# Second group's square sums, first state keys and last head factors placed later among the products; no products of zeros; last results stored by pairs of tiles

## The chip, the core and the metric

The kernel runs on one core of a Trainium2 chip. The metric is the device time of one execution in microseconds; the time of a kernel is the median of its runs. Every duration below comes from one profiled execution, from the runs' times, or from what the trace of that execution answers.

The core has five engines with a queue each: TensorE (PE in the profile; its weight loads are PEld), VectorE (DVE), ScalarE (ACT), GpSimd (POOL) and SyncE (SP). An instruction waits at the head of its engine's queue until what it needs is there, and what stands behind it waits with it.

## What is computed

A decoder trunk of two layers over 16 meta tokens and 512 tokens, model width 1024, in float32:

```python
for layer in range(DEPTH):
    g = norm_gains[layer]
    h = h + 0.5 * rmsnorm(swiglu(rmsnorm(h, g[0]), w_ffn_in[layer, 0], w_ffn_out[layer, 0]), g[1])
    hn = rmsnorm(h, g[2])
    if layer < N_A_LAYERS:
        mix = gla_mixer(hn, ...)                      # chunked gated linear attention, 4 heads
    else:
        mix = swa_mixer(hn, ..., k_sh, v_sh, cos, sin)  # sliding window of 128, 16 query heads, 4 key heads
    h = h + rmsnorm(mix, g[3])
    h = h + 0.5 * rmsnorm(swiglu(rmsnorm(h, g[4]), w_ffn_in[layer, 1], w_ffn_out[layer, 1]), g[5])
    if layer == N_A_LAYERS - 1:
        k_sh, v_sh = shared_kv(h, g_kv, w_kv, cos, sin)
return h[:, N_META:]
```

`rmsnorm` divides a row by the root of its mean square; `swiglu` is `(silu(gate) * up) @ w_out` with an inner width of 2816. The gated linear attention cumulates a gate per key channel, and each head's output goes through an `rmsnorm` of its own before it is gated and projected.

## The kernel before

**Layout.** Everything is held transposed: channels on the 128 partitions, tokens along the free dimension. The residual stream H and the work area Y are eight tiles of 128 channels by 528 tokens. Tokens come in two groups: in layer 0 `L0`, of 272 and 256 tokens; in layer 1 `L1`, of 256 and 256 (the meta tokens are dropped there), or `L1W`, one group of 512.

**Products.** A weight and an operand are each split into a high and a low float32r part, and a product is made of three matmuls: high by high, low by high, high by low. `mm3` (L344) does this for one output and `mm3s` (L333) for several outputs at once.

**Order of the work.** The program is written out by a small planner, `Flow` (L60). Jobs are Python generators; `yield 1.5` puts a job to sleep for 1.5 of the planner's clock. The clock moves with the products: `mm` (L161) adds n / 2400 for a float32r matmul of n columns and max(n / 600, 0.12) for any other. After a product, `flow.pump()` writes out each job that has come due. So a `yield` decides after how many products a job's instructions stand in TensorE's queue. A scheduler behind the planner may still exchange instructions that it takes to be not yet ready. `flow.wait` lets the clock run with no products until a job is done.

**Stages.** First FFN of layer 0 (names l0f0), gated linear attention (l0m), second FFN (l0f1), shared keys and values (kv), first FFN of layer 1 (l1f0), window attention (l1m), second FFN (l1f1), output. In the profile the figures at the end of names are left out, so the FFNs of a layer are both l0f or l1f.

**`x_first` (L509)** opens each stage: four weight units are multiplied by the first token group of the operand, then by the second, so that the second group's operand may come later. With at most 256 tokens in the group, two units share one PSUM bank of 512 columns. Before the products each such bank is set to zero by one matmul of a zero weight with a zero operand (L532), and none of the products starts an accumulation. Groups of 256 take two such matmuls, groups of 272 none: four in the stages of layer 1, two in the stages of layer 0 and in kv, 20 in all.

**Square sums and factors.** `Residual.run` (L453) ends a stage for one group: it makes the factors of the post-norm, adds the result to H tile by tile, builds the next operand from each tile and sums its squares (`sumsq`, ACT squares and POOL adds). Then L469 spawns `factors` (L436) for the next operand: `yield FACT`, and `rstd` (L348). `rstd` multiplies the sums by a column of ones (tile `st`), computes 1/sqrt on POOL or DVE into a diagonal matrix `dg`, sleeps for CHAIN (5) or DCHAIN (3.0), and multiplies ones by `dg` to spread the factors (tile `r`). `factors` copies `r` into R, by which the stage's outputs are scaled when they leave their banks (`drain`, L515).

**Gated linear attention (`gla`, L782).** One `core` job per head, each after the one before it. It prepares decayed queries and keys on DVE and ACT, sleeps for STATE_KEYS (L889) and transposes the state keys `kf` on TensorE (tile `pk`, L893). At its end `scale` (L951) makes the head's factors by `rstd` (tiles `st_go`, `dg_go`, `r_go`) for both groups. Between the heads' steps run the products of the next units; eight units of the output gate close the stage and the output projection follows.

**Window attention (`swa`, L1060).** Queries are scaled by R and rotated as they leave their banks; then score, softmax and value jobs run for eight pairs of heads, with four more query units and, later, the output projection between them.

**Output (`store`, L471).** For each group, four steps of two tiles: DVE multiplies by the factors, DVE or POOL adds H, and SP issues one store for each of the two tiles (L481, L482).

## Time and profile before

| | us |
|---|---|
| median of 3 runs | 1934.42 (1931.07 to 1936.41) |
| the profiled execution | 1931.38 |
| its span | 1929.5 |
| TensorE busy in it | 1888.9 |

The span is the time from the first to the last instruction that the profile shows; the execution's own time has 1.9 us more around it. The granted TensorE clock was 0.996 of full speed over the span. A row of TensorE's timeline that merges many matmuls gives the time from the first start to the last end; a single matmul's duration is its way through the array, and several are under way at once, so the pace is read from start to start.

### The profile page before, as it was taken

The numbers are of one execution on the slowest core, as the hardware profiler recorded it, in microseconds if no ns is written. First come the engines' busy times: TensorE is split into PE (matmuls) and PEld (weight loads), VectorE is DVE, ScalarE is ACT, GpSimd is POOL, SyncE is SP. The second block draws the span as 40 slices with busy tenths as digits, with TensorE's granted clock in tenths as the row PEclk, the third lists the DMA queues.
The fourth block names the chain that finished last, engine by engine and source line by source line (L and its number), as shares of the span: only waits on it lengthen the run. The fifth ranks groups of instructions, "written<-read, shape, count | busy, mean of one in ns | idle before, by whom it ended". The sixth has DMA issues, their size and how long they took to land.

```text
span 1929.5 us, 37402 instructions
## 1 busy us (share of the span) xinstructions
PE 1888.9 (98%) x14522; PEld 1798.1 (93%) x14522; DVE 1420.1 (74%) x2868; ACT 1001.7 (52%) x2268; POOL 215.1 (11%) x417
## 2 busy tenths in 40 slices
PE   8999999999999999999999999999998999999997
PEld 7999999999999999999999898989976898989897
DVE  7885858676464788585887786868788779858584
ACT  5663636653245555353574453535645665636363
POOL 2000000321111400000033000000352140000002
PEclk9999999999999999999999999999999999999998
DMA  4332333322113123323351123233421212333331
GB/s 163 104 100 88 103 96 106 114 74 69 45 52 113 56 72 95 102 91 102 99 176 45 61 88 115 87 112 99 132 66 34 77 45 72 98 105 107 101 112 44
DMA packets 102144, 174.61 MB, mean 90 GB/s; under 512 B 11472, under 2 KB 24272, under 8 KB 101968
## 3 DMA queue, kind: packets, MB, share of 16 engines
q1 hardware_dynamic: 101680, 172.11, 28.2%
q8 instruction: 113, 1.85, 0.4%
q14 instruction: 63, 0.52, 0.1%
q10 hardware_dynamic: 288, 0.13, 0.0%
HBM read 170.10 MB, written 2.10 MB: 89 GB/s over the span
## 4 chain that ended last, share of the span: by engine, by line
PE 70%; DVE 19%; ACT 6%; issue 3%; POOL 1%; DMA 0%; SPq 0%; DVEq 0%; ACTq 0%; POOLq 0%
PE y L162 30%; PE x L162 16%; PE a L162 11%; DVE raw L251 5%; PE c L162 4%; DVE w_s L246 3%; DVE w L246 3%; ACT w_s L245 3%; PE d L162 2%; DVE w L227 2%; PE o L162 1%; ACT w L226 1%; PE po L162 1%; DVE hidl0f L775 1%; PE sc L162 0%
## 5 line engine op out<-in xcount | busy, mean ns | idle before, releaser
L246 DVE TENSOR_TENSOR w_s<-raw,w_s 128x512 fp32r<-128x512 f32 x288 | 194.0, 690 | 129.7 <-ACT w_s L245 127.6
L227 DVE TENSOR_TENSOR w<-raw,w 128x512 fp32r<-128x512 f32 x378 | 244.9, 673 | 31.1 <-ACT w L226 29.3
L162 PE MATMUL y<-hidl0f,w 128*128 128x256 f32 (+1 forms) x2112 | 261.0, 285 | 0.0
L162 PEld LDWEIGHTS y<-hidl0f,w 128*128 128x128 f32 x2112 | 258.8, 188 | 0.7
L245 ACT ACTIVATE w_s<-raw 128x512 fp32r<-128x512 f32 x288 | 175.3, 628 | 149.5 <-DVE raw L251 146.0
L162 PE MATMUL y<-hidl1f,w 128*128 128x512 f32 (+1 forms) x1344 | 249.8, 346 | 0.0
L162 PEld LDWEIGHTS y<-hidl1f,w 128*128 128x128 f32 x1344 | 212.0, 188 | 33.9 <-ACT hidl1f L774 0.4
L226 ACT ACTIVATE w<-raw 128x512 fp32r<-128x512 f32 x378 | 209.0, 586 | 46.0 <-PE y L162 39.4
L403 POOL TENSOR_TENSOR acc_post<-acc_post,sq_post 128x256 f32<-128x256 f32 (+1 forms) x72 | 56.9, 791 | 1386.5 <-ACT sq_post L402 1386.0
L251 DVE TENSOR_TENSOR raw<-raw,raw 128x512 f32<-128x512 f32 x288 | 198.0, 687 | 5.5
L246 DVE TENSOR_TENSOR w<-raw,w 128x512 fp32r<-128x512 f32 x216 | 148.3, 687 | 41.5 <-ACT w L245 40.2
L245 ACT ACTIVATE w<-raw 128x512 fp32r<-128x512 f32 x216 | 133.9, 621 | 48.0 <-PE y L162 47.7
L162 PE MATMUL x<-x_l0m,w 128*128 128x272 f32 (+1 forms) x1200 | 158.3, 288 | 0.0
L162 PEld LDWEIGHTS x<-x_l0m,w 128*128 128x128 f32 x1200 | 149.4, 189 | 1.2
L572 DVE TENSOR_TENSOR Y<-y,Y 128x256 f32<-128x256 f32 (+2 forms) x176 | 83.0, 473 | 74.4 <-PE y L162 73.8
L162 PE MATMUL a<-zl0f_t,w_s 128*128 128x264 f32 x864 | 117.8, 285 | 3.8 <-ACT c L751 3.8
L162 PE MATMUL a<-zl1f_t,w_s 128*128 128x256 f32 x864 | 115.1, 282 | 2.0 <-ACT c L751 1.6
L162 PEld LDWEIGHTS a<-zl0f_t,w_s 128*128 128x128 f32 x864 | 110.1, 188 | 5.0 <-ACT c L751 5.0
L162 PEld LDWEIGHTS a<-zl1f_t,w_s 128*128 128x128 f32 x864 | 106.9, 188 | 4.8 <-ACT c L751 4.8
L162 PE MATMUL x<-x_l0f,w 128*128 128x256 f32 (+1 forms) x768 | 100.0, 290 | 7.5 <-ACT w L226 5.8
L162 PEld LDWEIGHTS x<-x_l0f,w 128*128 128x128 f32 x768 | 96.6, 191 | 8.9 <-ACT w L226 5.8
L162 PE MATMUL x<-x_l1f,w 128*128 128x256 f32 (+1 forms) x576 | 93.1, 320 | 0.0
(485 smaller groups left out, 3306.5 us busy)
## 6 DMA issues: line engine op xcount, KB each, us to landing
raw<-in_w_in SPq DMA_DIRECT2D x352, 256.0 KB, 2.9
raw<-in_w_out SPq DMA_DIRECT2D x96, 256.0 KB, 3.3
raw<-in_gla_in SPq DMA_DIRECT2D x50, 256.0 KB, 3.0
raw<-in_w_last SPq DMA_DIRECT2D x48, 256.0 KB, 3.1
raw<-in_w_out SPq DMA_DIRECT2D x64, 128.0 KB, 3.0
raw<-in_gla_out SPq DMA_DIRECT2D x16, 256.0 KB, 2.9
raw<-in_w_q SPq DMA_DIRECT2D x16, 256.0 KB, 3.6
raw<-in_swa_out SPq DMA_DIRECT2D x16, 256.0 KB, 2.8
```

The source lines that it names most:

```text
L162: inst = pe.matmul(o, lhs, rhs, start=start, stop=stop, skip_group_check=onto)
L226: act.activation(w[:, 0, :m], raw[:, :m], AF.Copy)
L227: dve.tensor_tensor(w[:, 1, :m], raw[:, :m], w[:, 0, :m].bitcast(F32), op=ALU.subtract)
L245: act.activation(w[:, 0, :512], src, AF.Copy)
L246: dve.tensor_tensor(w[:, 1, :512], src, w[:, 0, :512].bitcast(F32), op=ALU.subtract)
L251: dve.tensor_tensor(dst, dst, src, op=ALU.add)
L403: pool.tensor_tensor(sums[0][:, :n], sums[0][:, :n], t[:, :n], op=ALU.add)
L572: dve.tensor_tensor(y, p[:, :n], y, op=ALU.add)
L775: dve.scalar_tensor_tensor(t.hid[:, 1, g], t.h, -1.0, t.hid[:, 0, g].bitcast(F32), op0=ALU.mult, op1=ALU.subtract)
```

## The change

It has five parts.

- `BEHIND = 1.5` of the planner's clock. The factors of the second group (`gi` is 1) are spawned that much later (L469), for the five operands that a `Residual` builds: l0m, l0f1, kv, l1m and l1f1.
- The same delay is added before the state keys of head 0, and between `st_go` and `r_go` of head 3 (`h // 3` is 1 for it alone).
- The matmuls that set shared banks to zero are gone. The first product of the first unit in a bank starts the accumulation; the products of the second unit carry no start, and a flag (`skip_group_check`) lets them stand so in the program.
- Each unit's last product now carries a stop; before, only the second unit's did.
- The last results are stored by two tiles at a time, 256 KB each. SP issues them, but for the second and the fourth pair of the second group, which ACT issues.

```diff
+BEHIND = 1.5
...
     def mm3s(outs, j, x, g, start, stop, shared=False):
...
-        for o, w in outs:
-            mm(o, w[j // 4][:, 0, cols], xh, start and not shared, False)
-            mm(o, w[j // 4][:, 1, cols], xh, False, False)
         for i, (o, w) in enumerate(outs):
-            mm(o, w[j // 4][:, 0, cols], xl, False, stop and (not shared or i % 2 == 1))
+            second = shared and i % 2 == 1
+            mm(o, w[j // 4][:, 0, cols], xh, start and not second, False, second)
+            mm(o, w[j // 4][:, 1, cols], xh, False, False, second)
+        for i, (o, w) in enumerate(outs):
+            second = shared and i % 2 == 1
+            mm(o, w[j // 4][:, 0, cols], xl, False, stop, second)
             flow.pump()
...
-    def rstd(sq, n, dim, half, name, eng=pool):
+    def rstd(sq, n, dim, half, name, eng=pool, more=0.0):
...
-        yield DCHAIN if eng is dve else CHAIN
+        yield (DCHAIN if eng is dve else CHAIN) + more
...
-            nxt.rjob[gi] = flow.spawn(nxt.factors(gi))
+            nxt.rjob[gi] = flow.spawn(nxt.factors(gi), gi * BEHIND)
...
-                for j in (k, k + 1):
-                    sp.dma_start(out[j, :, o - META : o - META + n], H[:, j, o : o + n])
+                to = out[k : k + 2, :, o - META : o - META + n].rearrange("k p n -> p k n")
+                (act if gi and k % 4 else sp).dma_start(to, h)
...
                 banks = [ps(f"x{used[0]}_{i}_{gi}") for i in some[::2]]
-                for b in banks:
-                    mm(b.rearrange("p (a c) -> p a c", c=P), zeros, zeros.unsqueeze(1).to_broadcast([P, 4, P]), True, False)
...
-                yield STATE_KEYS
+                yield STATE_KEYS + (0 if h else BEHIND)
...
-                    r = yield from rstd(accs[gi], n, 256, True, f"go{h}_{gi}")
+                    r = yield from rstd(accs[gi], n, 256, True, f"go{h}_{gi}", more=h // 3 * BEHIND)
```

## The prediction

> **What bounds the kernel now.** I read the page first, then the waits of TensorE, then the timeline of TensorE around each place that the diff touches, then the busy time of each engine in the attention stage, and last the end of the trace.

> ```profile
> span 1929.5 us, 37402 instructions
> ...
> PE 1888.9 (98%) x14522; PEld 1798.1 (93%) x14522; DVE 1420.1 (74%) x2868; ACT 1001.7 (52%) x2268; POOL 215.1 (11%) x417
> ```

> TensorE is busy for 1888.9 of 1929.5 us, so 40.6 us are all that waiting can give. A microsecond of products that is taken out is worth a microsecond wherever the next stage is fed in time. The waits of TensorE (what it waited for: us in total, times, longest) name most of the 40.6 us:

> ```profile
> PE x L162 <- ACT w L226: 5.8, 1, 5.8
> ...
> PE r_post_out L162 <- DVE dg_post_out L383: 2.7, 1, 2.7
> PE sc L162 <- DVE pt L1157: 2.5, 1, 2.5
> PE sc L162 <- DVE Y L1117: 2.2, 2, 2.1
> ...
> PE r_go L162 <- POOL dg_go L383: 1.6, 1, 1.6
> PE sc L162 <- DVE q L1001: 1.3, 1, 1.3
> PE pk L174 <- DVE f L880: 1.3, 1, 1.3
> PE st_l1m L162 <- POOL acc_l1m L403: 1.1, 1, 1.1
> PE st_l0f L162 <- ACT acc_l0f L399: 1.1, 1, 1.1
> ...
> PE st_kv L162 <- POOL acc_kv L403: 0.7, 1, 0.7
> PE ptm L174 <- DVE mt L1135: 0.7, 1, 0.7
> ```

> Five of these rows are the moved steps: st_l0f, st_kv and st_l1m (square sums of the second group, taken by TensorE before their last addend is there), pk (state keys of head 0) and r_go (factors of the last head). The sums of l0m and l1f have no row: their delay gains nothing.

> **The products of zeros.** The timeline of TensorE (start, length, instruction, count, wait before it) at the first FFN's second half, and the group of the zero products:

> ```profile
> L162 PE MATMUL x<-zeros x20: 388/396/402, 23.3 to 1572.9; 128*128 128x512 f32 x20
> ```
> ```profile
> 653.42 0.63 PE L162 MATMUL x<-zeros 128*128 128x512 f32 x2
> 653.89 8.66 PE L162 MATMUL x<-x_l0f,w 128*128 128x256 f32 x72
> 662.39 0.28 PE L162 MATMUL st_l0f<-ones,acc_l0f 128*128 128x1 f32 x2
> 662.52 1.07 PE L162 MATMUL x<-x_l0f,w 128*128 128x256 f32 x7
> 664.67 0.83 PE L162 MATMUL st_l0f<-ones,acc_l0f 128*128 128x1 f32 x6 [1.07 <-ACT acc_l0f L399]
> ...
> 670.70 0.70 PE L162 MATMUL r_l0f<-dg_l0f,ones 128*128 128x256 f32 x2 [0.19 <-POOL dg_l0f L383]
> ```

> A zero product's 396 ns is its time through the array; what it costs is the distance to the next start: (653.89 − 653.42) / 2 = 0.235 us. No zero product stands behind a wait, so none is hidden: 20 × 0.235 = 4.7 us on TensorE. Their planner cost (512 / 2400 = 0.213 each) goes too, so jobs that are due at a time of the planner's clock now come out about two products later for each; those jobs keep their place in time and the products slip ahead of them.

> [...]

> **Square sums of the second group, 1.5 later.** BEHIND counts on the planner's clock, where a 256-column product is 256 / 2400 = 0.107. So 1.5 is 14 products, and at 8.66 / 72 = 0.120 us each 1.7 us of real work. With the 8 small products st also ACT's and POOL's chain, r and the copy into R move. At l0f the wait of 1.07 us is shorter than 1.7, so it goes whole, and r comes 1.7 − 1.07 = 0.6 us later; st_kv: 0.7 gone, r 1.0 later. What is behind R are the drains of the second group's banks. The 41 products between st and r_l0f run without a wait, and none after r is charged to a full bank, so I cost the lateness at nothing; if that cover were gone it is 0.6 and 1.0. Gain 1.07 + 0.7 = 1.8 us.

> At l1m it is different. TensorE's sums and factors, and DVE's first work behind them:

> ```profile
> 1407.99 0.63 PE L162 MATMUL x<-zeros 128*128 128x512 f32 x2
> ...
> 1418.22 0.38 PE L162 MATMUL st_l1m<-ones,acc_l1m 128*128 128x1 f32 x2 [1.13 <-POOL acc_l1m L403]
> ...
> 1424.84 0.59 PE L162 MATMUL r_l1m<-dg_l1m,ones 128*128 128x256 f32 x2
> ```
> ```profile
> 1425.89 0.76 DVE L1081 SCALAR_TENSOR_TENSOR csq<-csq,R_l1m 128x256 f32<-128x256 f32 x2 [3.42 <-ACT R_l1m L442]
> ```

> DVE stood idle for 3.42 us until R_l1m came, and from there it is the engine that bounds attention (busy us per stretch, then the granted clock):

> ```profile
> core 0: us, PE busy (x) PEld busy (x) DVE busy (x) ACT busy (x) POOL busy (x), PEclk, DMA share, GB/s
> 1425.90:1440.00 14.10, 12.80 (x57) 7.62 (x56) 14.10 (x28) 7.85 (x22) 9.88 (x10) 1.00 0.30 96
> 1440.00:1455.00 15.00, 12.10 (x58) 7.51 (x58) 14.17 (x48) 10.71 (x47) 4.15 (x4) 1.00 0.25 85
> 1455.00:1470.00 15.00, 14.23 (x107) 10.30 (x106) 12.88 (x41) 7.24 (x35) 2.55 (x3) 0.89 0.12 37
> 1470.00:1490.00 20.00, 17.25 (x176) 13.28 (x171) 18.41 (x45) 10.46 (x40) 5.28 (x5) 1.00 0.11 34
> ...
> 1490.00:1500.00 10.00, 10.00 (x47) 6.96 (x46) 7.21 (x30) 8.74 (x44) 1.82 (x2) 1.00 0.12 42
> ```

> From 1425.9 to 1490 DVE is busy for 59.6 of 64.1 us and TensorE for 56.4; only after 1490 is TensorE full again. What TensorE gains in this stage before 1426 (four zero products, 0.94, and the wait of 1.13) is therefore waited away by 1490. Worse, r_l1m comes 1.7 − 1.13 = 0.6 later, and with it the whole DVE stretch: a loss of 0.6. Hence 16 zero products count, 16 × 0.235 = 3.8 us.

> **State keys of head 0 and factors of the last head.** In the gated linear attention:

> ```profile
> 435.33 0.66 PE L174 MATMUL pk<-ident,f 128*128 128x128 f32 x4 [1.25 <-DVE f L880]
> ```
> ```profile
> 570.24 1.54 PE L162 MATMUL r_go<-dg_go,ones 68*128 68x272 f32 x4 [1.56 <-POOL dg_go L383]
> 571.43 18.61 PE L162 MATMUL x<-x_l0m,w 128*128 128x272 f32 x150
> ```

> pk placed 1.7 us later no longer waits: 1.25 gained. Behind pk on TensorE the products of the next units stand, which need nothing of it. For r_go, 1.7 us of products go ahead of it; the wait was 1.56, and inside the 1.54 us the second pair waits on POOL too, so I take 1.6. The delays add up for the chain of heads: 1.7 (second factors of l0m) + 1.7 (pk) + 1.7 (r_go) = 5.1 us later against the products. Behind r_go are 150 products, 18.6 us, before the output projection needs the heads; that covers 5.1. Without this cover they would cost the 5.1.

> **The stores.** The end of the trace on POOL, SP's queue and DVE, and the DMA issues (size, us to landing):

> ```profile
> 1921.85 2.49 POOL L480 TENSOR_TENSOR H<-t_out,H 128x512 f32<-128x512 f32 x2 [6.79 <-DVE t_out L479]
> 1923.14 4.00 SPq L482 DMA_DIRECT2D out<-H  x8
> 1923.48 1.28 DVE L480 TENSOR_TENSOR H<-t_out,H 128x512 f32<-128x512 f32 x2
> ```
> ```profile
> raw<-in_w_in SPq DMA_DIRECT2D x352, 256.0 KB, 2.9
> ...
> out<-H SPq DMA_DIRECT2D x16, 128.0 KB, 1.8
> H<-in_h SPq DMA_DIRECT2D x4, 256.0 KB, 5.5
> ```

> Eight issues fill 4.00 us, about 0.45 each, so the last starts near 1926.7 and lands 1.8 later, at 1928.5; the span ends 1.0 after that. With pairs, SP and ACT issue two each. The data are ready at 1921.85 + 2.49 = 1924.3 (POOL's second pair, on ACT's queue) and 1923.48 + 1.28 = 1924.8 (DVE's second, behind it on ACT). The only instruction behind ACT's waiting store is its other store, which starts near 1924.8. No 256 KB store is in the trace. With 1.8 us to landing it ends at 1926.6, a gain of 1.9; with the two-run loads of H at the start, 5.5, at 1930.3, a loss of 1.8. I take 2.9, the loads of this size, as nearest: 1927.7, a gain of 0.8. The first group's stores lie under products.

> **The sum.** 3.8 + 1.8 + 1.25 + 1.6 + 0.8 − 0.6 = 8.6 us. The profiled execution took 1931.38, so 1922.8; it lies 3.0 below the median of the runs, 1934.42, and on the median's scale the forecast is 1925.8.

> **Rivals.** (a) Attention isn't held by DVE: the 4.5 us that DVE has free in it take up the shift. Then 0.94 + 1.13 + 0.6 come back: 11.2 gained, 1923.2. Against it is DVE's full 14.10 of 14.10 at the start.

> (b) The planner's order isn't the engine's order: the eight st_l0f stand split 2 and 6, with seven products between, so something behind the planner reorders. If it puts the moved steps back, or the later factors hold up DVE by as much, the 1.8 + 1.25 + 1.6 of the moves are lost: 4.0 gained, 1930.4.

> (c) The clock. After the wait of 2.2 us in attention the granted clock fell:

> ```profile
> 1457.00:1459.00 2.00, 1.71 (x8) 1.22 (x8) 2.00 (x8) 0.29 (x1) 0.00 (x0) 0.52 0.79 250
> 1459.00:1461.00 2.00, 2.00 (x22) 1.49 (x20) 2.00 (x7) 0.47 (x2) 0.00 (x0) 0.62 0.06 20
> ```

> That took 0.48 × 1.71 + 0.38 × 2.00 = 1.6 us of work. The wait of 2.5 us before 1490 was not followed by a drop (1.00). If products run ahead and it grows by 0.94 + 1.13 + 0.6 = 2.7, a drop there would hit the place where TensorE becomes the bound: 7.0 gained, 1927.4. [...]

> (d) Slower: attention loses its cover. The place is the four large waits of it (2.5, 2.2, 1.3, 0.7); the 2.7 us of products that now run ahead are missing at each. If each grows by 2.7 and they don't overlap, that is 10.8, with a clock drop in two of them 3.2 more: 1925.8 + 14.0 = 1939.8. It decides from R_l1m's arrival on, and needs DVE's order to get worse, since DVE's work stays the same; nothing in the stretch shows that.

> **How the numbers follow.** About 0.3%, 5.8 us, is what can be told from no change. Forecast 0.50 (of it 0.44 faster, 0.06 within), (a) 0.15 (0.14, 0.01), (b) 0.17 (0.04 faster, 0.12 within, 0.01 slower), (c) 0.10 (0.08, 0.02), (d) 0.08 (at 5.4 above the median it sits on the line: 0.04 within, 0.04 slower): faster 0.70, same 0.25, slower 0.05. Low end: (a) less 2.7 for the store's better end and the spread of a median, 1920.5. High end: (b) with the store's worse end, 1930.4 + 2.6 = 1933.0. (d) stays outside.

> **What would show it.** x<-zeros is gone and st_l0f, st_kv, st_l1m, pk and r_go have no row or under 0.3 in TensorE's waits; sc's waits in attention are longer by 2 to 3 us in all; the last store lands 0.5 to 1.2 us sooner after the last product. The forecast is wrong if products after 1490 start over 1.5 us sooner against r_l1m, or if a wait over 1 us stands where none did.

## The result, and the profile after

| | before | after |
|---|---|---|
| median of 6 runs, us | 1935.17 (1931.07 to 1936.41) | 1943.55 (1938.77 to 1944.23) |
| the profiled execution, us | 1931.38 | 1943.72 |
| its span, us | 1929.5 | 1941.8 |
| its mean granted TensorE clock | 0.996 | 0.990 |

The change made the kernel slower: the ratio of the runs is 1.0038 (1.0028 to 1.0049) and the medians are 8.4 us apart, where 1925.8 and a gain of 8.6 were forecast. The two profiles lie further apart (12.3 us) than the medians, because the profiled execution of before is one of those with the highest granted clock (0.996): in 43 of the 59 runs of it beside the later experiments the granted clock was 0.993, and their median 1935.7. So about 4 us of what the two profiles differ by belong to these two executions. The ratios below leave out two later executions far from all others, 7527.03 us of the kernel with the scans held back and 2040.96 of the kernel before; the medians include them.

The page of after, its first lines, and the waits of TensorE (what it waited for: us in total, times, longest):

```profile
span 1941.8 us, 37350 instructions
...
PE 1897.7 (98%) x14502; PEld 1805.5 (93%) x14502; DVE 1418.7 (73%) x2868; ACT 1002.2 (52%) x2268; POOL 223.0 (11%) x417
```
```profile
PE r_go L163 <- POOL dg_go L387: 6.2, 3, 2.3
...
PE ptm L175 <- DVE mt L1137: 5.7, 3, 2.6
...
PE sc L163 <- DVE Y L1119: 1.3, 1, 1.3
PE x L163 <- ACT x_l1m L429: 1.3, 1, 1.3
...
PE pk L175 <- DVE f L882: 0.2, 1, 0.2
```

The waits that the change aimed at are gone: st_l0f, st_kv and st_l1m have no row, and pk has 0.2. But r_go now waits three times for 6.2 us, where it waited once for 1.6, and in attention x_l1m and ptm have taken the place of st_l1m and sc. TensorE is also busy for 8.8 us more, although 20 products are gone.

Where both come from is seen when the span is cut into stages. The busy time of each engine and the granted clock, over the gated linear attention (from the first l0m product to the output projection), and over the window attention (from the first l1m product to the next FFN), before and then after:

```profile
379.64:589.87 210.23, 207.29 (x1674) 199.24 (x1673) 126.27 (x278) 84.17 (x186) 36.08 (x136) 1.00 0.20 60
1394.02:1559.08 165.06, 156.22 (x1173) 126.75 (x1172) 130.92 (x356) 94.78 (x329) 54.61 (x77) 0.99 0.16 52
```
```profile
378.47:597.71 219.24, 212.41 (x1673) 203.35 (x1671) 126.47 (x278) 84.89 (x186) 43.68 (x136) 0.98 0.19 57
1398.76:1572.50 173.74, 162.97 (x1171) 131.66 (x1169) 129.71 (x356) 95.03 (x327) 54.93 (x77) 0.95 0.16 49
```

The first figure behind the stretch is its length, the next TensorE's busy time. The gated linear attention grew by 9.0 us: idle time from 2.94 to 6.83 (+3.9), busy time by 5.1 at a lower clock (the same products, run slower). Attention grew by 8.7: idle from 8.84 to 10.77 (+1.9), busy by 6.75. So in these two executions the two stages lost 17.7 us, 5.8 of it as waits and 11.9 as lowered clock, and the rest of the kernel won 5.4. POOL is busy for 7.6 us more in the first stage (36.08 to 43.68) with the same 136 instructions.

The waits at r_go first. The timeline of POOL and then of DVE at head 0's factors, before:

```profile
456.36 0.20 POOL L367 TENSOR_TENSOR zv_go<-zv_go,av_go 128x2 f32<-128x2 f32 x1
456.51 0.20 POOL L369 TENSOR_TENSOR wv_go<-wv_go,zv_go 68x4 f32<-68x4 f32 x1
456.79 0.19 POOL L368 TENSOR_SCALAR wv_go<-zv_go 128x2 f32<-128x2 f32 x1
457.06 0.23 POOL L376 TENSOR_SCALAR wv_go<-wv_go 68x4 f32<-68x4 f32 x1
```
```profile
459.52 0.78 DVE L816 TENSOR_TENSOR qk<-x,R_l0m 128x272 f32<-128x272 f32 x2 [6.98 <-PE x L162]
460.23 1.45 DVE L852 TENSOR_TENSOR_SCAN b<-resets,ls 128x528 f32<-128x528 f32 x1
```

The same places after, with TensorE's wait as the last:

```profile
457.72 0.59 POOL L371 TENSOR_TENSOR zv_go<-zv_go,av_go 128x2 f32<-128x2 f32 x1
458.27 0.64 POOL L373 TENSOR_TENSOR wv_go<-wv_go,zv_go 68x4 f32<-68x4 f32 x1
459.00 1.02 POOL L372 TENSOR_SCALAR wv_go<-zv_go 128x2 f32<-128x2 f32 x1
460.10 1.10 POOL L380 TENSOR_SCALAR wv_go<-wv_go 68x4 f32<-68x4 f32 x1
```
```profile
456.89 0.78 DVE L818 TENSOR_TENSOR qk<-x,R_l0m 128x272 f32<-128x272 f32 x2 [5.58 <-PE x L163]
457.58 1.28 DVE L228 TENSOR_TENSOR w<-raw,w 128x512 fp32r<-128x512 f32 x2
458.78 1.25 DVE L854 TENSOR_TENSOR_SCAN b<-resets,ls 128x528 f32<-128x528 f32 x1
459.95 1.23 DVE L855 TENSOR_TENSOR_SCAN b<-resets,ls 128x528 f32<-128x528 f32 x1
```
```profile
463.69 2.06 PE L163 MATMUL r_go<-dg_go,ones 68*128 68x272 f32 x4 [2.10 <-POOL dg_go L387]
```

Before, DVE was idle for 6.98 us while POOL worked out the factors, and then drained a unit (qk) and ran the next head's scans. After, the heads' chain stands 31 products later among the same products (474 products of l0m's units stand ahead of head 0's st_go, before 443; at 0.12 us each that is 3.7 us), the unit is ready in the middle of the chain, and behind its drain DVE goes on with weight splits (L228) and both scans. The four POOL operations that run beside these take 0.59, 0.64, 1.02 and 1.10 us instead of 0.19 to 0.23; under the drain, which reads PSUM, POOL's operations kept their 0.19 to 0.20. The four lose 2.5 us. Between st_go and r_go TensorE has the same 42 products as before, so a chain that is longer by this ends in a wait of 2.10.

And behind the wait the clock falls. The busy time of stretches of 3.41 us around it (the same columns):

```profile
457.29:460.70 3.41, 3.41 (x31) 3.41 (x30) 3.41 (x6) 0.42 (x1) 3.08 (x6) 1.00 0.38 112
460.70:464.11 3.41, 1.31 (x10) 0.97 (x8) 0.48 (x1) 0.21 (x1) 3.25 (x15) 1.00 0.13 46
464.11:467.52 3.41, 3.41 (x14) 2.71 (x13) 1.97 (x4) 0.88 (x2) 0.36 (x1) 0.50 0.00 0
467.52:470.94 3.42, 3.42 (x30) 3.38 (x30) 2.73 (x6) 3.42 (x8) 0.00 (x0) 1.00 0.00 0
```

In the stretch of the wait TensorE was busy for 1.31 of 3.41 us; in the next it was granted half the clock and did 14 matmuls, where the stretch behind it, at full clock again, has 30. Heads 1 and 2 repeat it, with half clock from 505.0 and 546.0: three stretches of 3.41 us at half speed cost 5.1 us, which is the growth of the busy time.

In attention the opening changed:

```profile
1424.09 1.22 PE L163 MATMUL x<-x_l1m,w 128*128 128x256 f32 x8 [1.29 <-ACT x_l1m L429]
1425.14 0.50 PE L163 MATMUL st_l1m<-ones,acc_l1m 128*128 128x1 f32 x4
1425.89 0.39 PE L163 MATMUL x<-x_l1m,w 128*128 128x256 f32 x1 [0.24 <-DVE x_l1m L430]
...
1426.47 7.70 PE L163 MATMUL x<-x_l1m,w 128*128 128x256 f32 x27
1434.01 0.59 PE L163 MATMUL r_l1m<-dg_l1m,ones 128*128 128x256 f32 x2
```

With the sums moved back, TensorE runs into the operand's last tiles, which are not built yet. r_l1m comes 1434.01 − 1398.76 = 35.25 us after the stage's first product, before 1424.84 − 1394.02 = 30.82: 4.4 later, where 0.6 was forecast; one stretch at half clock, from 1426.65, lies in between. 17.07 us of the stage run at half clock, before 3.41.

The DMA issues of the results on ACT's queue (size, median us to landing):

```profile
out<-H ACTq DMA_DIRECT2D x2, 256.0 KB, 2.9
```

They take the 2.9 us that the prediction chose for them. From the start of the last product to the end are 13.80 us, before 14.49: 0.7 gained, as forecast (0.8).

### The profile page after: what moved, and what is told of

Its sections match the earlier page's. It is cut to its first block, busy times and chain, and to the rows that moved or that the text cites. A ratio compares the mean times of both kernels' runs of the same rounds, so it can differ in the third digit from the quotient of the medians.

```text
span 1941.8 us, 37350 instructions
## 1 busy us (share of the span) xinstructions
PE 1897.7 (98%) x14502; PEld 1805.5 (93%) x14502; DVE 1418.7 (73%) x2868; ACT 1002.2 (52%) x2268; POOL 223.0 (11%) x417
## 3 DMA queue, kind: packets, MB, share of 16 engines
q8 instruction: 113, 1.85, 0.4%
## 4 chain that ended last, share of the span: by engine, by line
PE 68%; DVE 20%; ACT 6%; issue 3%; POOL 2%; DMA 0%; SPq 0%; DVEq 0%; ACTq 0%; POOLq 0%
PE y L163 30%; PE x L163 16%; PE a L163 10%; DVE raw L252 5%; DVE w_s L247 4%; PE c L163 3%; ACT w_s L246 3%; DVE w L247 3%; PE d L163 2%; DVE w L228 1%; PE o L163 1%; PE po L163 1%; ACT w L227 1%; DVE hidl1f L777 1%; DVE hidl0f L777 1%
## 5 line engine op out<-in xcount | busy, mean ns | idle before, releaser
L228 DVE TENSOR_TENSOR w<-raw,w 128x512 fp32r<-128x512 f32 x378 | 243.1, 669 | 30.7 <-ACT w L227 28.7
## 6 DMA issues: line engine op xcount, KB each, us to landing
raw<-in_w_in SPq DMA_DIRECT2D x352, 256.0 KB, 2.9
raw<-in_w_out SPq DMA_DIRECT2D x96, 256.0 KB, 3.3
raw<-in_gla_in SPq DMA_DIRECT2D x50, 256.0 KB, 3.0
raw<-in_w_last SPq DMA_DIRECT2D x48, 256.0 KB, 3.0
raw<-in_w_out SPq DMA_DIRECT2D x64, 128.0 KB, 2.9
raw<-in_gla_out SPq DMA_DIRECT2D x16, 256.0 KB, 2.7
raw<-in_w_q SPq DMA_DIRECT2D x16, 256.0 KB, 3.6
raw<-in_swa_out SPq DMA_DIRECT2D x16, 256.0 KB, 2.9
```

The lines of the kernel that those rows point to most:

```text
L228: dve.tensor_tensor(w[:, 1, :m], raw[:, :m], w[:, 0, :m].bitcast(F32), op=ALU.subtract)
```

## The experiments

Two readings were open at first. In the gated linear attention the change moves three things of the chain of heads (the factors of l0m and the state keys, 1.7 us each, and the last head's r_go) and takes two products of zeros out. Either the shift of the chain makes the loss, or the missing products do. Each kernel is the changed one with the edit shown; the ratios are to the kernel before, whose median beside them was 1935.1 to 1935.5.

**One shift taken back.**

```diff
-                yield STATE_KEYS + (0 if h else BEHIND)
+                yield STATE_KEYS
```

> The changed kernel with head 0's state keys placed as before (STATE_KEYS alone), all else changed. In the changed kernel the gated linear attention takes 219.2 us from its first product to the first product of the output projection (210.2 before), with waits for r_go of 2.1, 2.3 and 1.9 us at heads 0 to 2, each followed by 3.41 us of half clock. Theory A (the heads' chain was moved 3.4 us against the units by two delays of 1.7, and DVE's work for the next head now falls on POOL's chain of factors and stretches it): with one delay left the overlap is half; the waits for r_go fall to under 1 us each, at most one half-clock stretch is left in the stage, the stage takes 210 to 214 us and the kernel 5 to 9 us less than the changed one. Rival B (the products run ahead because the products of zeros are gone, and that alone brings the waits): the stage stays at 218 to 220 us.

```diff
-            nxt.rjob[gi] = flow.spawn(nxt.factors(gi), gi * BEHIND)
+            nxt.rjob[gi] = flow.spawn(nxt.factors(gi), gi * BEHIND * (self.name not in ('l0m',)))
```

> The changed kernel with the second group's factors of l0m spawned without delay, the state keys' delay kept. Theory A: the same as without the state keys' delay, since both are 1.7 us of the one shift: waits for r_go at heads 0 to 2 under 1 us each, the stage 210 to 214 us, the kernel 5 to 9 us less than the changed one; the wait of pk stays away. Rival B (products of zeros): 218 to 220 us in the stage. Rival C (only the state keys' delay matters, as it sits inside the heads' chain): 217 us or more.

Without the keys' delay: 1936.11 us, ratio 1.0008 (0.9999 to 1.0017). Without l0m's: 1936.38, ratio 1.0003 (0.9992 to 1.0014). Either brings back most of the loss, but the waits do not fall under 1 us, as had been expected: r_go still waits 1.58, 1.54, 0.44 and 1.49 at the four heads in the first, and 1.52, 1.59, none and 0.24 in the second. What went is most of the clock's part: no half-clock stretch in the stage in the first (length 214.26) and one in the second (212.64). In the first, TensorE's idle time in the stage is 6.97 us, no less than the changed kernel's 6.83 (pk waits 1.69 again), and yet the stage is 5.0 shorter. Waits of 1.5 were cheaper here than waits of 2.1 by more than their difference.

**No shift at all: zeros and stores alone.**

```diff
-            nxt.rjob[gi] = flow.spawn(nxt.factors(gi), gi * BEHIND)
+            nxt.rjob[gi] = flow.spawn(nxt.factors(gi))
...
-                yield STATE_KEYS + (0 if h else BEHIND)
+                yield STATE_KEYS
...
-                    r = yield from rstd(accs[gi], n, 256, True, f"go{h}_{gi}", more=h // 3 * BEHIND)
+                    r = yield from rstd(accs[gi], n, 256, True, f"go{h}_{gi}", more=0.0)
```

> The kernel before with only the products of zeros taken out and the last results stored by pairs; no delay anywhere. By the prediction's terms 16 x 0.235 = 3.8 us and 0.6 for the stores (the two spans from the last product differ by about that) are gained: 1931 by the median. Theory A: no wait for r_go over 0.3 us at heads 0 to 2, the gated linear attention 209.8 us. Rival B (products running ahead bring the waits): waits for r_go of about 2 us at heads 0 to 2 and a stage of 214 us or more. In attention: if the delay at l1m is what lost there, the stage from the first product of l1m to the first of l1f1 takes 164 to 166 us (165.1 before, 173.7 changed); if the missing products of zeros are, 168 or more.

1936.24 us, ratio 1.0007 (0.9997 to 1.0017), where 1931 was expected. The gated linear attention is 209.78 long (before 210.24), with the one wait for r_go of before. So the missing zeros do not make its loss; the shifts do. But zeros and stores together, forecast at 4.6, gain nothing. TensorE's waits in this kernel, the rows that grew or are new against before (and st_l0f, which had 1.1):

```profile
PE st_l1m L163 <- POOL acc_l1m L407: 3.1, 1, 3.1
...
PE st_kv L163 <- POOL acc_kv L407: 1.1, 1, 1.1
PE st_l0f L163 <- ACT acc_l0f L403: 1.0, 1, 1.0
PE r_kv L163 <- POOL dg_kv L387: 1.0, 1, 1.0
...
PE r_l1f L163 <- POOL dg_l1f L387: 0.8, 1, 0.8
PE r_l0f L163 <- POOL dg_l0f L387: 0.8, 1, 0.8
```

The three r rows, each for a POOL result, had 0.2, none and 0.2 before, st_kv 0.7 and st_l1m 1.1. With the zeros gone, TensorE comes earlier to sums and factors that are not ready: in the five stages from the second FFN on its idle time is longer by 0.53, 0.43, 0.58, 2.00 and 0.77, together 4.3 us, for 16 zero products that took 16 × 0.235 = 3.8. In attention the wait of 3.1 is followed by 6.83 us at half clock, and the stage takes 172.43 instead of 165.06.

In attention something else changed with the zeros, which their 0.94 us do not show: the order on POOL. POOL's last additions of the square sums, before and then here:

```profile
1416.12 2.04 POOL L403 TENSOR_TENSOR acc_l1m<-acc_l1m,sq_l1m 128x256 f32<-128x256 f32 x2
```
```profile
1413.43 1.17 POOL L407 TENSOR_TENSOR acc_l1m<-acc_l1m,sq_l1m 128x256 f32<-128x256 f32 x1
1414.57 0.90 POOL L1004 TENSOR_TENSOR sh_q<-sh_q,csq 128x256 f32<-128x256 f32 x1
1415.55 1.05 POOL L1005 TENSOR_TENSOR q<-q,sh_q 128x256 f32<-128x256 f32 x1
1416.56 0.72 POOL L407 TENSOR_TENSOR acc_l1m<-acc_l1m,sq_l1m 128x256 f32<-128x256 f32 x1
```

Before, the two additions stand next to each other; here two steps of a query's rotation stand between them. The last addition ends 25.63 us after the stage's first product (1391.65), before 24.14 after it (1394.02). So TensorE's wait for it grew by 2.0, where the two zero products between that first product and the sums are worth 0.47. The changed kernel has the same order, and where the zeros are put back (below) the two additions are together again. Whether the zeros' 0.94 us or their share of the planner's clock matters more has no run of its own.

**The sums of l1m at their old place, the zeros still gone.**

```diff
-            nxt.rjob[gi] = flow.spawn(nxt.factors(gi), gi * BEHIND)
+            nxt.rjob[gi] = flow.spawn(nxt.factors(gi), gi * BEHIND * (self.name not in ('l1m',)))
```

> The changed kernel with the second group's factors of l1m spawned without delay, the other four delayed. The attention stage (first product of l1m to first of l1f1) took 165.1 us before and 173.7 changed, with half clock in 17 us of it against 3.4. Theory D (r_l1m 4.4 us later sets it all, DVE and the softmax chain start from it, and waits behind drop the clock): the stage takes 165 to 167 us and the kernel 7 to 9 us less than the changed one. Rival E (the operand of l1m isn't built in time since the products of zeros are gone; the new wait of 1.29 us for x_l1m drops the clock first): the wait stays and the stage takes 169 us or more.

1940.37 us, ratio 1.0027 (1.0016 to 1.0037), 3.2 under the changed kernel, where 7 to 9 were expected if the delay set it all. The three waits for r_go stand as in the changed kernel. In attention the wait for the operand is gone and st_l1m waits 3.10 again; the stage is 172.13, 1.6 shorter than in the changed kernel, and r_l1m still comes 35.40 us after the stage's first product. The delay alone is thus not what makes attention slow; the missing zeros are left.

**What stretches POOL's chain.** Two kernels went at the waits for r_go in different ways: one lets more products run ahead of every r_go, the other leaves TensorE's order as it is and only holds DVE's scans back.

```diff
-                    r = yield from rstd(accs[gi], n, 256, True, f"go{h}_{gi}", more=h // 3 * BEHIND)
+                    r = yield from rstd(accs[gi], n, 256, True, f"go{h}_{gi}", more=BEHIND)
```

> The changed kernel with the 1.5 of the last head's factors given to all four heads, so that 14 more products (1.7 us) stand ahead of each r_go. If the loss in the gated linear attention is the three waits for r_go (2.10, 2.26, 1.88 us) and the half clock behind them, each wait falls by 1.7 to under 0.6, no half-clock stretch is left in the stage, and its length goes from 219.2 to 210-213 us; time 1934-1938. If the chain of heads has no slack, the waits only move to pk, pa or the next head's r_go and the stage stays above 216; time 1940-1944.

```diff
+            scaled = {}
...
-                dve.tensor_tensor_scan(b64, m64, lg, 0.0, op0=ALU.mult, op1=ALU.add)
-                dve.tensor_tensor_scan(b128, m128, lg, 0.0, op0=ALU.mult, op1=ALU.add)
+                for m, b in ((m64, b64), (m128, b128)):
+                    scan = dve.tensor_tensor_scan(b, m, lg, 0.0, op0=ALU.mult, op1=ALU.add)
+                    for s in scaled.values():
+                        after(s, scan)
...
-                    dve.tensor_tensor(
+                    scaled[gi] = dve.tensor_tensor(
                         yy[:, :, o : o + n], yy[:, :, o : o + n],
```

(`after` sets an order between two instructions of one engine, with no wait.)

> The changed kernel with one thing more: VectorE takes a head's two scans only behind the scaling of the head before (TensorE's order is untouched). Theory: the scans, running while POOL works out the head's factors, stretch POOL's small operations from 0.19 to 0.6-1.1 us. Then these are back at 0.2-0.4, the waits for r_go at heads 0 to 2 fall from 2.10, 2.26, 1.88 to under 1.0 each, no half-clock stretch follows them, the stage is 209-213 us long instead of 219.2, and the time is 1934-1938. Rival: POOL's chain is late by its place alone; then the waits stay over 1.5, the stage over 217, the time over 1941. A third way: the scans' lateness makes the next head late and a new wait of over 1 us stands at pk or pa.

Later r_go: 1930.19 us, ratio 0.9966 (0.9952 to 0.998), below the 1934 to 1938 expected; the waits for r_go are 0.26 and less but for 0.38 at the last head, a wait of 0.97 for the last head's pk is new, and the stage is 208.59 long. Scans held back: 1933.44 us, ratio 0.9987 (0.9978 to 0.9997). POOL, TensorE and the stage's row with the scans held back:

```profile
457.28 0.59 POOL L371 TENSOR_TENSOR zv_go<-zv_go,av_go 128x2 f32<-128x2 f32 x1
457.83 0.65 POOL L373 TENSOR_TENSOR wv_go<-wv_go,zv_go 68x4 f32<-68x4 f32 x1
458.56 0.19 POOL L372 TENSOR_SCALAR wv_go<-zv_go 128x2 f32<-128x2 f32 x1
458.83 0.23 POOL L380 TENSOR_SCALAR wv_go<-wv_go 68x4 f32<-68x4 f32 x1
```
```profile
461.55 1.54 PE L163 MATMUL r_go<-dg_go,ones 68*128 68x272 f32 x4 [0.40 <-POOL dg_go L387]
```
```profile
378.04:588.25 210.21, 207.67 (x1672) 199.05 (x1671) 125.81 (x278) 84.95 (x186) 39.32 (x136) 1.00 0.19 60
```

The two operations that ran beside the scans are back from 1.02 and 1.10 to 0.19 and 0.23; the two beside the splits keep 0.59 and 0.65. The wait falls from 2.10 to 0.40, the clock stays at 1.00, and the stage is 9.0 us shorter than in the changed kernel. TensorE's matmuls stand in the same order as in the changed kernel, so taking DVE's scans out of the chain's way gives back all that the stage lost against before, though not yet what it was to gain. Heads 1 and 2 (0.48, 0.95) go the same way. The kernel without l0m's delay (above) and the last one below are the same comparison once more, as in this stage they differ by the scans alone: r_go's waits of 1.52 and 1.59 are gone, TensorE's idle time falls from 3.88 to 0.55 and the length from 212.64 to 207.13.

**The zeros of attention put back.** In both, the delay of the state keys and of l0m's sums is taken out as above; the first takes out l1m's as well.

```diff
+                if x.name == "l1m":
+                    for b in banks:
+                        mm(b.rearrange("p (a c) -> p a c", c=P), zeros, zeros.unsqueeze(1).to_broadcast([P, 4, P]), True, True)
                 pst = [banks[i // 2][:, i % 2 * 256 : i % 2 * 256 + n] for i in range(len(some))]
```

> The changed kernel with the four products of zeros of the window attention's opening put back, and without the later sums of l0m and l1m and the later first state keys; the later sums of l0f1, kv and l1f1, the last head's later factors and the stores stay. Theory: in attention the zero products are cover for POOL's last addition; with them the wait at st_l1m is near 1.1 again and the stage with its output projection is 165-167 us (changed kernel 173.7, zeros alone removed 172.4). The gated linear attention is 208-210 us. Time 1927-1931, faster than the kernel before (1935.4). Rival: what moves ahead of attention (products, loads) sets its length, not the zeros; then it stays at 170-174 and the time is 1933-1937.

> The kernel of the run before this one (zeros back in attention's opening) with the later sums of l1m kept. If only the missing zeros hurt attention, it is 164-167 us long, as without the delay, and the time 1926-1931. If the later sums hurt by themselves (R_l1m 0.6 us later by the prediction, 1.7 at most), it is 167-172 and the time 2-6 us above the other run's.

Without l1m's delay 1926.48 us, ratio 0.9951 (0.9936 to 0.9966); with it 1929.80, ratio 0.9975 (0.9964 to 0.9986). In the first, st_l1m waits 1.13 as before, and attention is 167.68 long; in the second x_l1m waits 1.41 and attention is 168.55. Splitting each length into waits, the time at half clock (of which half is lost where TensorE doesn't wait within it) and the rest, which is the length less the waits and half of that time:

| kernel | length | waits | at half clock | rest |
|---|---|---|---|---|
| before | 165.06 | 8.84 | 3.41 | 154.51 |
| after | 173.74 | 10.77 | 17.07 | 154.43 |
| zeros and stores alone | 172.43 | 10.84 | 17.07 | 153.06 |
| l1m's delay out | 172.13 | 9.95 | 20.48 | 151.94 |
| zeros back, no delay | 167.68 | 8.72 | 10.24 | 153.84 |
| zeros back, with delay | 168.55 | 9.43 | 6.83 | 155.71 |

Four zero products take 0.94 us; in this table, where the delay is the same, the rest is lower without them by 0.8 to 2.6. With them the waits go back from 10.84 to 8.72, and less time is lost to the clock in both kernels. How much less is the looser part of this: the time at half clock is one execution's for each kernel, and the column spreads from 3.41 to 10.24 for the same waits (before, and zeros back).

Other kernels of the study do the same work in this stage, and show how far one execution can be trusted. Without zeros and with the delay there are five: 169.83 to 176.12 long, with waits of 9.44 to 10.77. Without both there are two (172.43 and 172.13), and with zeros and no delay four: 165.06 to 168.44, with waits of 8.50 to 8.84. Both lengths and waits of these four lie below all of the seven without zeros: that the missing zeros hurt is shown, but not by how much to the microsecond.

That the later sums cost by themselves shows in the medians (1929.80 against 1926.48) and in waits plus rest (165.14 against 162.56). Of r_l1m's place, too, both have a share: 30.81 us after the stage's first product with zeros and no delay, 34.18 with zeros and delay, 35.40 with neither.

**Both mends.** The scans are held back, and attention has its zeros back and its sums at their old place; the second kernel also leaves l0m's sums at theirs.

> The changed kernel with two mends: VectorE's scans behind the scaling of the head before, and at the window attention the four products of zeros back and its sums at their old place. If the two losses found so far (POOL's stretched chain in the gated linear attention, the missing cover at l1m) are the whole of the difference, the gated linear attention is 208-211 us (changed kernel 219.2), attention with its output projection 163-168 (173.7), and the time 1925-1930, against 1943.6 for the changed kernel and 1935.3 for the one before. If something else of the change costs, it stays at 1933 or more.

> As the run beside it, but without the later sums of l0m: the delays of the state keys and of the last head's factors stay. The wait at pk is 0.2 instead of the 1.25 of the kernel before and of the kernel with zeros back, and the scans cannot stretch POOL's chain, so the gated linear attention should be 207-209 us and the time 1924-1928. If l0m's later sums cost nothing of their own, both runs agree within 2 us.

1928.86 us, ratio 0.9965 (0.9952 to 0.9977), and 1925.20, ratio 0.9946 (0.9933 to 0.9959). With the two mends the changed kernel is 6.7 us faster than the one before; without l0m's later sums it is 10.3 us faster, the best kernel of the study. Its gated linear attention:

```profile
378.42:585.55 207.13, 206.58 (x1672) 198.86 (x1671) 126.34 (x278) 84.34 (x186) 36.07 (x136) 1.00 0.20 61
```

0.55 us of idle time is left in a stage that had 2.94. l0m's later sums do cost by themselves: 210.24 against 207.13 in this stage, and 3.7 us in the medians, where agreement within 2 had been expected. The waits for r_go are part of it: 0.41, 0.48 and 0.92 at heads 0 to 2 with the later sums, under 0.15 without. The rest of the 3.1 stays open.

## Why the prediction was wrong, point by point

**The step that failed first** is the sentence on the chain of heads: "Behind r_go are 150 products, 18.6 us, before the output projection needs the heads; that covers 5.1." It looked for what needs the heads' results, at the end of the last head. That cover did hold: 102 products were left behind the last r_go, and the output projection waited for nothing. It did not look at what the shift brings together on the way. The chain of each head, POOL's factors among it, moved against the units' products, and DVE's work hangs on those: its drains, and the splits and scans that the scheduler lets in behind them. Before, head 0's chain on POOL fell, but for its last steps, into 6.98 us in which DVE was idle. The head that already showed the danger was the last, whose 1.56 us wait the prediction quoted as a thing to be removed without asking why this head alone waited: there, in the kernel before, eight of POOL's small operations take 0.31 to 0.73 us, beside the gating and splits that DVE runs from 564.2 to 568.0. Holding the scans back shows the cause: POOL's two operations beside them go from 1.02 and 1.10 us to 0.19 and 0.23, and 9.0 us of stage are regained. The lateness of the heads' chain, which the prediction held covered and so put at nothing, measured 9.0 in the profiled executions: 3.9 of waits, 5.1 of clock.

In the changed kernel, at head 0, POOL's operations took 0.59 to 1.10 us under the splits and scans, and 0.19 to 0.20 under the drain from PSUM.

**The second** is the l1m term: "What TensorE gains in this stage before 1426 … is therefore waited away by 1490", with a loss of 0.6. That the gain would be waited away was right. That nothing would be lost beyond it was wrong: TensorE, early, stood 3.1 us at st_l1m, or 1.3 at the operand where the sums were moved, and the clock fell behind such waits (6.83 us at half clock behind the first, 3.41 behind the second). r_l1m came 4.4 later, and attention lost 8.7 in place of 0.6. The term of 0.6 was too small even for the delay alone: with the zeros in place it brings r_l1m 3.4 later (34.18 against 30.81), and TensorE waits 1.41 for the operand.

**The zeros** were sized wrongly: 16 × 0.235 = 3.8 was counted because "no zero product stands behind a wait, so none is hidden". True of the zeros themselves, but products after them do wait, on sums and factors that come no sooner for it. Removed alone, 3.8 us of them came back as 4.3 us of waits. The prediction did say that their share of the planner's clock goes too, but priced no change of order by it; in attention two steps of POOL came to stand ahead of its last addition.

**Right** were these. pk: 1.0 gained (1.25 to 0.24), forecast 1.25; the stage shows it once the scans are held back (208.19 with zeros back, 207.13 in the last kernel). The last head's factors: with no shift of the chain the stage went from 209.78 (zeros and stores alone) to 208.19 (zeros back, where the last r_go is later): 1.6, as forecast. The second group's sums of l0f1 and kv: between the same two kernels l0f1 went from 372.64 to 370.77 and kv from 28.44 to 25.63, while the FFN after kv took 1.85 more: 2.8 in all, against a forecast of 1.8. The two aren't quite the same thing, as the 2.8 also takes back waits that the missing zeros had brought there (r_kv, r_l0f). The stores: 0.7 of 0.8.

**The rivals.** The slower one (d) named attention, one of the two stages: it did lose cover, but its waits grew by 1.9 in all, not by 2.7 each. It asked for a worse order on DVE; the one that got worse was POOL's. The clock rival (c) named half clock behind a wait and expected one drop of 1.6 us in one place; it was 11.9 us in two stages of the profiled execution. The sign set down beforehand, "a wait over 1 us stands where none did", came true at heads 0 to 2. That the best kernel, at 1925.20, stands where the forecast stood is no support for it: that kernel leaves out two of the moves, keeps four of the zero products and holds the scans back.

## What to carry to other kernels

A step that is placed later moves its whole chain against everything that hangs on the products: list what the other engines do in the place where each part of the chain will fall, not only who waits at its end. Work that looks useless ahead of a wait (here products of zeros) may be the cover of that wait; price its removal by the wait that comes next, and move that with it. Where a planner counts such work, its removal also changes the order on other engines, so compare their queues too. A wait of about 2 us was dearer here than it looks, for the clock behind it cost up to 1.7 us more.

## What the runs showed of the hardware

| busy share | stretches | next at half clock |
|---|---|---|
| under 0.50 | 24 | 24 |
| 0.50 to 0.62 | 19 | 10 |
| 0.62 to 0.75 | 49 | 2 |
| over 0.75 | about 6500 | 1 |

In the profiles of before and after alone the last column is 4 of 4, 2 of 3, 1 of 13 and none of 1091.

So a wait of about 1.5 us was followed by no half clock in one kernel, and in another by a stretch of it, which costs 3.41 / 2 = 1.7 us of work. The kernel without the keys' delay has such a stretch, with a wait of 1.58 in it and no drop behind it; the kernel without l0m's delay, shown second, has one with a wait of 1.52 and a drop:

```profile
459.51:462.93 3.42, 1.84 (x14) 1.62 (x14) 1.78 (x2) 0.21 (x1) 3.26 (x9) 1.00 0.00 0
462.93:466.34 3.41, 3.29 (x24) 2.76 (x24) 1.92 (x3) 1.66 (x4) 0.53 (x1) 1.00 0.02 5
```
```profile
459.29:462.70 3.41, 1.89 (x10) 1.36 (x11) 1.54 (x3) 0.21 (x1) 2.11 (x6) 1.00 0.02 5
462.70:466.11 3.41, 3.41 (x18) 3.41 (x18) 2.33 (x5) 2.84 (x6) 0.00 (x0) 0.50 0.12 19
```

TensorE was busy for 1.84 of 3.42 us (0.54) in the one, and the clock stayed at 1.00, and for 1.89 of 3.41 (0.55) in the other, and it was halved, as it was behind the changed kernel's 1.31 of 3.41 (0.38). What decides between 0.50 and 0.62 isn't shown. One kernel's runs spread over 6 us with its clock (the kernel before: median 1935.7 at 0.993, 1930.9 at 0.996). That is why one profile's clock should not be taken for the kernel's.

**POOL beside DVE.** Of the small operations of the heads' factor chains in the changed kernel, the 58 that ran with DVE idle or draining PSUM (L818, L971) have a median of 0.19 us, the 12 beside a weight split (L228) or the gating (L412, L973, L978) one of 0.39 (0.19 to 0.59), and the six beside the scans alone one of 1.04 (up to 1.14). The two beside the scans of head 0 end at 459.00 + 1.02 = 460.02 and 460.10 + 1.10 = 461.20, the scans at 458.78 + 1.25 = 460.03 and 459.95 + 1.23 = 461.18: each within 0.02 us of the scan beside it.
